# Two-layer hybrid encoder trunk on one Trainium2 core: residual quarters loaded one a unit from GpSimd's queue, every second early gate/up weight through other buffers, the second meta substitution placed later

## The chip, the cores and the metric

The kernel runs on one core of a Trainium2 chip. The metric is the device time of one execution in microseconds (us). Engines are named as in the profile: PE is TensorE (matmul; PEld its weight loads), DVE is VectorE, ACT is ScalarE, POOL is GpSimd, SP is SyncE, which here only issues DMAs. DMAs are issued from three queues: SP's (nearly all), ACT's, and POOL's. [...]

## The reference, cut to what matters

Sixteen learned meta tokens are put ahead of 1024 tokens, so that the sequence has L = 1040 columns; the model width is 1024. Two layers follow:

```python
for l in range(DEPTH):
    h = h + hybrid_mixer(rmsnorm(h, norm1_w[l]), w_in[l], conv_qkv_w[l], ...)
    h = h + swiglu(rmsnorm(h, norm2_w[l]), w_gate_up[l], w_down[l])
h = rmsnorm(h, final_norm_w)
return h[:, N_META:]
```

The mixer has a bidirectional gated-delta-rule part (4 heads of 128, worked in chunks, which needs the inverse of a triangular matrix for each chunk, head and direction) and a gated short convolution. SwiGLU is `(silu(h @ gate) * (h @ up)) @ w_down` with an inner width of 2816 = 22 tiles of 128. All inputs are float32.

## The kernel before, in words

**Precision and layout.** Activations lie transposed, channels on the 128 partitions and tokens along the free axis. Each float32 operand of a large product is split into a high part (a rounded copy made by ACT) and a low part (the difference, made by DVE or POOL), and three matmuls are added up: high x high, high x low, low x high. Such a triple stands at L157 to L159 (`dense`), L1021 to L1023 (`prod`, for gate/up) and L1441 to L1443 (down projection).

**The planner.** The kernel is written in a framework that allots buffers, sets semaphores and plans the order of each engine's list: it goes through a simulated timeline with modelled durations and picks by priority among what is ready. Priorities follow the order of the program except where the kernel sets them itself. Tiles with a tag share a fixed number of buffers: `raw` has 2 (weights just loaded), `whi` and `wlo` 3 each (split weights), `ck2` has 5 (tiles of 2 KB a partition for many uses). A tile waits until one of its buffers has been released. `after(ins, prev)` adds a dependency by hand.

**Mixer.** While the query projections run, `chunk_p` (L442) computes for each of nine chunks c the decayed k-k products of both directions d, and `k_out` (L418) transposes k for the chunk on PE (L424), copies it into a `ck2` tile `kt` on ACT (L426) and stores it (L427). One `k_out` and one `chunk_p` are worked after each third of a projection. For chunk 0, the 16 meta tokens, the triangular system is solved by `meta()` (L464): a store to DRAM and two loads on SP (L468 to L470), 30 small operations on POOL (L474 and L475), and a store and a load on SP (L476 and L477). It holds two `ck2` tiles. Layer 0 has one for each direction, both at chunk 0; layer 1 needs only d = 0. `query_lengths` (L608) sends sums through DRAM into the `ck2` tile `rows` with POOL DMAs (L617, L618), and PE transposes it.

**Output projection and early gate/up.** The output projection goes over 8 row tiles in two halves of the columns (`out_part`, L947), its weights loaded through `raw`. The gate/up product is a Strassen-like scheme with seven products for four blocks. Two of the products of the first four of 22 tiles f are worked early, during and after the output projection: `early_part(f, q)` (L1047) loads a weight of 256 KB into a `raw` tile (L1050), splits it (L1003 on ACT, L1004 on DVE) and multiplies. Besides these, DVE then forms sums of the normalised activations (L983) and their low parts (L971).

**Gate/up.** For each f four weights are loaded, two into `raw` and two into `ck2` (L1288 to L1291), and combined on DVE (L1296 to L1301).

**Down projection.** Also with seven products (P5, P3, P2, P1, P6, P7, P4), worked in 84 units (p, b, m): for each product, three blocks b of three inner tiles, and four row tiles m. A unit has 9 triples' worth of matmuls: 18 matmuls of 260 columns in layer 0, 9 of 512 in layer 1. Weights are prepared five units ahead (`LEAD`, L1202, L1203, with sums at L1160 and L1199), activations are loaded back from DRAM (L1222) into a ring of seven parts and split (L1250, L1251; a difference at L1253). Many DVE operations are tied behind the addition of two units earlier (`behind`). After the last block a product is added to the residual `hr` (L1447), which must have been loaded by then: the quarter (a row tile's half of the columns, 256 or 260 KB) is loaded from `hd` at L1421, in the units with b = 1 of the products P5, P3, P2 and P7: 16 loads a layer, which have no dependency but the room and go out on SP as soon as the planner finds a place.

Of the kernel before, what the change touches and what calls it, by code (L numbers as in the profile page):

```python
# [17 lines left out]
L = 1040  # L18
# [24 lines left out]
def trunk(ctx: ExitStack, tc: tile.TileContext, xT, w_in, w_ba, w_out, w_gu, w_dn,  # L43
          par_d, alog_d, dtb_d, cst_d, eye_d, out):
    nc = tc.nc
# [16 lines left out]
    def t2k(tag):  # L62
        return sb.tile([128, 4, 128], F32, tag="ck2", bufs=5, name=nm(tag))
# [25 lines left out]
    def after(ins, prev):  # L89

        if prev is not None:
            tc.add_manual_dep(ins.ins, prev.ins.name, dep, reason="order")
        return ins
# [4 lines left out]
    mm = nc.tensor.matmul  # L98
# [5 lines left out]
    dma = nc.sync.dma_start  # L104
    adma = nc.scalar.dma_start
    qdma = nc.gpsimd.dma_start
# [125 lines left out]
    for m in range(KT):  # L232
        cs = FULL if m == 0 else [(0, L)]
# [46 lines left out]
    for l in range(DEPTH):  # L280
# [6 lines left out]
        o0 = 16 if last else 0  # L287
# [32 lines left out]
        hd = dram.tile([KT, 128, L], F32, name=nm("hd"))  # L320
# [117 lines left out]
            return (16, 0) if c == 0 else (128, 16 + 128 * (c - 1))  # L438

        ptm = []  # L440

        def chunk_p(c):  # L442

            if not Pd:
                Pd.extend(sb.tile([128, 4 * L], F32, tag=f"P{d}", name=nm("P")) for d in range(2))
                Pv.extend(p[:, 0:4096].rearrange("p (q i) -> p q i", i=128) for p in Pd)
                p_ = sb.tile([128, 4 * L], F32, tag=Y[0][2], name=nm("ptm"))
                ptm.extend(p_[:, 512 * i:512 * i + 512].rearrange("p (h i) -> p h i", h=4) for i in range(8))
            n, s0 = span(c)
            kk = bank("b").rearrange("p (h i) -> p h i", h=4)  # L450
            for h in range(H):
                mm(kk[0:n, h, 0:n], KTt[:, h, s0:s0 + n], KTt[:, h, s0:s0 + n], start=True, stop=True)
            for d in (dirs0 if c == 0 else (0, 1)):
                gr = ptm[(2 * c + d) % 8]
                adma(gr[0:n, :, 0:n], gd[36 * d + 4 * c:36 * d + 4 * c + 4, 0:n].partition_broadcast(n))
                for h in range(H):
                    stt(out=gr[0:n, h, 0:n], in0=gr[0:n, h, 0:n], scalar=nGb[0:n, d, c, h:h + 1], in1=off[0:n, d, 0:n], op0=ALU.subtract, op1=ALU.add)
                act(out=gr[0:n, :, 0:n], in_=gr[0:n, :, 0:n], func=AF.Exp, scale=-1.0)
                adma(dtd[c, d].rearrange("p (h i) -> p h i", h=4)[0:n, :, 0:n], gr[0:n, :, 0:n])
                dst = P0[d] if c == 0 else Pv[d][:, 4 * c - 4:4 * c, :]  # L460
                tt(out=dst, in0=kk[0:n, :, 0:n], in1=gr[0:n, :, 0:n], op=ALU.mult)
                if c == 0:

                    def meta():  # L464
                        mt = t2k("mt").rearrange("p a b -> p (a b)")[0:4].rearrange("p (w a b) -> p w a b", w=2, a=16)
                        Wm, Zm = mt[:, 0], mt[:, 1]
                        Tm = t2k("mt").rearrange("p a b -> p (a b)")[0:4, 0:256].rearrange("p (a b) -> p a b", a=16)
                        dma(m0d[d, 0].rearrange("h j i -> j h i"), P0[d])  # L468
                        dma(Wm, m0d[d, 0])
                        dma(Zm, eye_d[0:4, :, :][:, 0:16, 0:16])  # L470
                        for s in (range(15, 0, -1) if d == 0 else range(0, 15)):
                            r0, r1, a0, a1 = (0, s, s, 16) if d == 0 else (s + 1, 16, 0, s + 1)
                            sh = [4, r1 - r0, a1 - a0]
                            ptt(out=Tm[:, r0:r1, a0:a1], in0=Wm[:, r0:r1, s:s + 1].to_broadcast(sh), in1=Zm[:, s:s + 1, a0:a1].to_broadcast(sh), op=ALU.mult)  # L474
                            ptt(out=Zm[:, r0:r1, a0:a1], in0=Zm[:, r0:r1, a0:a1], in1=Tm[:, r0:r1, a0:a1], op=ALU.subtract)  # L475
                        dma(m0d[d, 1], Zm)  # L476
                        dma(P0[d], m0d[d, 1].rearrange("h j i -> j h i"))  # L477

                    meta()

        def chunk_a(c):

# [125 lines left out]
        def query_lengths(l2):  # L608


            r4 = t2k("r4").rearrange("p a b -> p (a b)")[:, 0:260]
            nc.vector.tensor_copy(r4, l2[:, 0:260])
            for h in range(H):
                qdma(rnd[h].rearrange("(a c) -> a c", a=4), r4.rearrange("(a b) c -> a b c", b=32)[:, h, :])
            rows = t2k("rows").rearrange("p a b -> p (a b)")[0:36, 0:128]
            for h in range(H):
                qdma(rows[9 * h:9 * h + 1, 0:16], rnd[h:h + 1, 0:16])  # L617
                qdma(rows[9 * h + 1:9 * h + 9, :], rnd[h, 16:L].rearrange("(c p) -> c p", p=128))  # L618

            def turn():  # L620
                ps = pa()
                low(lambda: nc.tensor.transpose(ps[:, 0:36], rows, ident[0:36, 0:36]))
                ts(out=g[:, 0].rearrange("p c h -> p h c"), in0=ps[:, 0:36].rearrange("p (h c) -> p h c", h=4), scalar1=HD * EPS, scalar2=HD * EPS * EPS, op0=ALU.mult, op1=ALU.add)

            jobs.append(turn)
# [258 lines left out]
        for i, (d, s) in enumerate(order):  # L884
            at_prio(base - 17000 + 4000 * (1 - d) + 400 * s)
            c = s if d == 0 else 8 - s
# [7 lines left out]
        hr = [hb[m // 4][:, m % 4, :] for m in range(KT)]  # L894
# [43 lines left out]
        def half(ap, z):  # L938

            v = ap.rearrange("p (g e) -> p g e", g=4) if len(ap.shape) == 2 else ap.rearrange("p k (g e) -> p k g e", g=4)  # L940
            s = slice(1, 3) if z == 0 else slice(0, 4, 3)
            return v[:, s, :] if len(ap.shape) == 2 else v[:, :, s, :]
# [70 lines left out]
        CW = E if E * 4 > 1024 else NB  # L1013
# [11 lines left out]
        def raw4(tag):  # L1025
            if tag == "raw":
                return wp.tile([128, WK, 128], F32, tag="raw", bufs=2, name=nm("raw"))
            return t2k("rw")
# [17 lines left out]

        def early_part(f, q):  # L1047

            A = raw4("raw")
            dma(A, w_gu[l, f, 0, :, 4 * q:4 * q + 4, :])  # L1050
            w = w_op(A, True)
            if q == 0:
                early[f] = (row(Y[1], F32, 3), row(X[1], F32, 3)) if f < 3 else (row(Y[1] + "f"), c4k())
                bks0[f] = [pbank() for j in range(NJ)]
            for j in range(NJ):
                prod(bks0[f][j], w, T[("B11", "B21")[q]], j, q == 0)
                act(out=part(early[f][1 - q], 0, j), in_=pin(bks0[f][j]), func=AF.Copy)  # L1057
# [12 lines left out]
        for m in range(KT + 2):  # L1070
# [7 lines left out]
            k = m - 2  # L1078
# [9 lines left out]
            else:  # L1088
                c = pcol(P_N2 + k)
# [171 lines left out]
        for t in range(4, NP * 7):  # L1261
            u = max(0, 4 * (t // 3 - 1) - 1 + t % 3)
# [23 lines left out]
        for f in range(FT):  # L1286
# [21 lines left out]
            g, u = early[f] if f < NE else (row((X[1], Y[1])[f % 2] + "f"), row(X[1], F32, 3))  # L1308
            ps = {}
# [99 lines left out]
              "P6": (0, 1, ALU.add), "P7": (1, 1, ALU.add), "P4": (1, 0, ALU.add)}  # L1409

        FIRST = {"P2": (0, 0), "P5": (1, 1), "P3": (0, 1), "P7": (1, 0)}
        bks = {}
        for i in range(NF):
            u = (42, 44, 46, 70)[i]
            under[u - 3].append(lambda i=i: plain_load(i))
            under[u].append(lambda i=i: plain_row(i))
        for u, (p, b, m) in enumerate(UNITS):
            if b == 1 and p in FIRST:
                dh, z = FIRST[p]
                q = 4 * dh + m  # L1420
                dma(half(hr[q][:, o0:L], z), half(hd[q][:, o0:L], z))  # L1421
            at[0] = u
            for fn in under[u]:
                fn()
            if last and u == 77:
                for q in range(KT):
                    last_weights(q)
            if not last and u >= len(UNITS) - 2:
                pre["dn", u - len(UNITS) + 2] = wload(w_dn[l, u - len(UNITS) + 2, :, 0:NF, :], NF)
            if p in ("P5", "P2", "P1") and b == 0:  # L1430
                for j in range(NJ):
                    bks[m, j] = pbank()
            wh, wl = dw.pop(("w", u))
            for j in range(NJ):
                ps = bks[m, j]
                cs = slice(CW * j, CW * j + CW)
                for k in range(3):
                    th, tl = t_slot(3 * (u // 4) + k)
                    st = p in ("P2", "P5", "P1") and b == 0 and k == 0
                    en = b == NBK - 1 and k == 2  # L1440
                    mm(ps[:, :CW], wh[:, k, :], th[:, cs], start=st, stop=False, skip_group_check=True)  # L1441
                    mm(ps[:, :CW], wh[:, k, :], tl[:, cs], start=False, stop=False, skip_group_check=True)  # L1442
                    mm(ps[:, :CW], wl[:, k, :], th[:, cs], start=False, stop=en, skip_group_check=True)  # L1443
                if b == NBK - 1:
                    dh, z, op = TO[p]
                    h = part(hr[4 * dh + m], z, j)
                    read_out[u] = tt(out=h, in0=pin(ps), in1=h, op=op)  # L1447
# [136 lines left out]
```

## Time and profile before

| | |
|---|---|
| median of 3 runs | 2505.1 us (2501.76 to 2505.31) |
| the profiled execution | 2502.22 us |
| its span, first to last instruction | 2500.1 us |
| granted TensorE clock, mean | 0.997 |
| DMA over the span | 335.26 MB, mean 134 GB/s |

A profile shows one execution. "Busy" is the time in which an engine worked on an instruction; the waits list gives for each group of instructions who released it, the total in us, how often, and the longest. In a list of DMAs the time to landing goes from issue to the last byte. The table of windows gives the busy us of each engine in a stretch of time, with the number of instructions in brackets, then the granted clock of PE (1 is full), the busy share of the 16 DMA engines, and GB/s.

### The profile page before, as it was taken

The numbers are of one execution on the slowest core, as the hardware profiler recorded it, in microseconds if no ns is written. First come the engines' busy times: TensorE is split into PE (matmuls) and PEld (weight loads), VectorE is DVE, ScalarE is ACT, GpSimd is POOL, SyncE is SP. The second block draws the span as 40 slices with busy tenths as digits, with TensorE's granted clock in tenths as the row PEclk, the third lists the DMA queues.
The fourth block names the chain that finished last, engine by engine and source line by source line (L and its number), as shares of the span: only waits on it lengthen the run. The fifth ranks groups of instructions, "written<-read, shape, count | busy, mean of one in ns | idle before, by whom it ended". The sixth has DMA issues, their size and how long they took to land. (4 is left out here: it accounts for less than half of the span.)

```text
span 2500.1 us, 44874 instructions
## 1 busy us (share of the span) xinstructions
PE 2461.5 (98%) x17508; PEld 2257.4 (90%) x17508; DVE 1693.0 (68%) x3073; ACT 1045.0 (42%) x1944; POOL 339.3 (14%) x359
## 2 busy tenths in 40 slices
PE   8999999999999999999999999999999999999998
PEld 6989999999999999999999888998978888887887
DVE  4788333659877777877656893336698777678765
ACT  5554333535333333344444543335453333234444
POOL 2031212431000000000120212132400000000012
PEclk9999999999999999999999999999999999999999
DMA  3444353523323332764224443445342233238531
GB/s 130 134 166 152 119 163 135 201 85 130 117 102 103 109 102 82 253 200 138 84 86 139 160 145 127 151 134 206 118 133 97 89 115 116 92 114 272 178 119 68
DMA packets 199529, 335.26 MB, mean 134 GB/s; under 512 B 23404, under 2 KB 85668, under 8 KB 199316
## 3 DMA queue, kind: packets, MB, share of 16 engines
q1 hardware_dynamic: 171204, 293.84, 35.3%
q10 hardware_dynamic: 25936, 34.19, 4.2%
q0 software_dynamic: 2176, 4.36, 0.5%
q8 instruction: 137, 2.24, 0.4%
q14 instruction: 76, 0.62, 0.1%
HBM read 250.31 MB, written 81.99 MB: 133 GB/s over the span
## 5 line engine op out<-in xcount | busy, mean ns | idle before, releaser
L131 POOL TENSOR_TENSOR wlo<-raw,whi 128x512 fp32r<-128x512 f32 x132 | 176.5, 1339 | 1267.8 <-ACT whi L130 1125.9
L157 PE MATMUL pacc<-a,whi 128*128 128x346 f32 (+1 forms) x808 | 264.5, 330 | 8.3 <-ACT whi L130 7.4
L159 PE MATMUL pacc<-a,wlo 128*128 128x346 f32 (+1 forms) x808 | 263.5, 327 | 1.1 <-POOL wlo L131 0.6
L157 PE MATMUL pacc<-b,whi 128*128 128x346 f32 (+2 forms) x672 | 234.5, 349 | 0.7 <-ACT whi L130 0.7
L159 PE MATMUL pacc<-b,wlo 128*128 128x346 f32 (+2 forms) x672 | 232.4, 347 | 0.9 <-DVE wlo L131 0.8
L158 PE MATMUL pacc<-a,whi 128*128 128x346 f32 (+1 forms) x688 | 225.8, 328 | 0.0
L158 PE MATMUL pacc<-b,whi 128*128 128x346 f32 (+2 forms) x580 | 200.7, 346 | 0.4 <-DVE b L907 0.3
L130 ACT ACTIVATE whi<-raw 128x512 fp32r<-128x512 f32 x168 | 105.8, 630 | 221.6 <-PE pacc L158 105.5
L157 PEld LDWEIGHTS pacc<-a,whi 128*128 128x128 f32 x808 | 152.8, 190 | 13.6 <-ACT whi L130 7.9
L159 PEld LDWEIGHTS pacc<-a,wlo 128*128 128x128 f32 x808 | 153.3, 190 | 2.6 <-POOL wlo L131 1.1
L157 PEld LDWEIGHTS pacc<-b,whi 128*128 128x128 f32 x672 | 126.4, 188 | 12.4 <-issue 3.1
L159 PEld LDWEIGHTS pacc<-b,wlo 128*128 128x128 f32 x672 | 126.3, 188 | 10.6 <-DVE wlo L131 1.0
L158 PEld LDWEIGHTS pacc<-a,whi 128*128 128x128 f32 x688 | 130.6, 190 | 2.9 <-issue 2.6
L158 PEld LDWEIGHTS pacc<-b,whi 128*128 128x128 f32 x580 | 109.2, 188 | 8.0 <-issue 0.9
L1003 ACT ACTIVATE whi<-rw 128x512 fp32r<-128x512 f32 x92 | 57.6, 631 | 137.7 <-PE pf L1022 36.4
L1003 ACT ACTIVATE b<-rw 128x512 fp32r<-128x512 f32 x64 | 39.9, 631 | 135.2 <-PE pacc L1022 37.7
L296 DVE TENSOR_TENSOR a<-pacc,rstd 128x346 f32<-128x346 f32 (+2 forms) x59 | 32.7, 555 | 85.4 <-PE pacc L159 85.4
L131 POOL TENSOR_TENSOR a<-raw,a 128x512 fp32r<-128x512 f32 x3 | 3.9, 1287 | 595.0 <-ACT a L130 595.0
L1003 ACT ACTIVATE a<-rw 128x512 fp32r<-128x512 f32 x64 | 40.0, 629 | 101.8 <-PE pacc L1022 62.3
L296 DVE TENSOR_TENSOR b<-pacc,rstd 128x346 f32<-128x346 f32 (+1 forms) x63 | 32.5, 515 | 72.5 <-PE pacc L159 72.5
L1004 DVE TENSOR_TENSOR wlo<-rw,whi 128x512 fp32r<-128x512 f32 x92 | 62.8, 685 | 2.9 <-ACT whi L1003 2.1
L1021 PE MATMUL pacc<-b,whi 128*128 128x260 f32 (+1 forms) x172 | 52.7, 306 | 0.7 <-ACT b L1057 0.7
(966 smaller groups left out, 8010.7 us busy)
## 6 DMA issues: line engine op xcount, KB each, us to landing
raw<-in_w_in SPq DMA_DIRECT2D x112, 256.0 KB, 2.9
raw<-in_w_gu SPq DMA_DIRECT2D x104, 256.0 KB, 3.0
rw<-in_w_gu SPq DMA_DIRECT2D x88, 256.0 KB, 3.1
rw<-in_w_dn SPq DMA_DIRECT2D x94, 192.0 KB, 2.7
rec<-vkd SPq DMA_DIRECT2D x61, 256.0 KB, 2.8
raw<-in_w_out SPq DMA_DIRECT2D x48, 256.0 KB, 2.7
b<-ad SPq DMA_DIRECT2D x45, 260.0 KB, 3.4
a<-ad SPq DMA_DIRECT2D x45, 256.0 KB, 5.2
```

Of the source, the lines that this page charges most:

```text
L130: whi_done[0] = act(out=hi, in_=raw[:, 0:kk, :], func=AF.Copy)
L131: (tt if lov[0] else ptt)(out=lo, in0=raw[:, 0:kk, :], in1=hi.bitcast(F32), op=ALU.subtract)
L157: mm(ps[:, :n], wh, xh[:, n0:n1], start=(k == 0), stop=False)
L158: mm(ps[:, :n], wh, xl[:, n0:n1], start=False, stop=False)
L159: mm(ps[:, :n], wl, xh[:, n0:n1], start=False, stop=(k == K - 1))
L296: tt(out=t[:, n0:n1], in0=ps, in1=rstd[:, n0:n1], op=ALU.mult)
L1003: act(out=hi, in_=src, func=AF.Copy)
L1004: tt(out=lo, in0=src, in1=hi.bitcast(F32), op=ALU.subtract)
L1021: mm(ps[:, :CW], w[0][:, k, :], th[:, cs], start=first and k == 0, stop=False, skip_group_check=True)
```

## The change

1. The residual quarters are issued from POOL's queue instead of SP's, and the one of unit u waits (by a dependency added by hand) for the first matmul of unit u - 2.
2. `early_part` loads the weights with q = 1 into a `ck2` tile instead of a `raw` tile: four of eight in each layer.
3. In layer 0 `meta()` for d = 1 is worked after chunk 5 instead of at chunk 0; that for d = 0 comes after both directions of chunk 0. In layer 1 the one that there is stays at chunk 0.
4. The tile `rows` is set to zero by POOL before it is filled.

```diff
         ptm = []
+        metas = []
...
-                    def meta():
+                    def meta(d=d):
...
-                    meta()
+                    metas.append(meta)
+            if c in (0, 5) and metas:
+                metas.pop(0)()
...
             rows = t2k("rows").rearrange("p a b -> p (a b)")[0:36, 0:128]
+            nc.gpsimd.memset(rows, 0.0)
...
         def early_part(f, q):
-            A = raw4("raw")
+            A = raw4(("raw", "ck2")[q])
...
-        bks = {}
+        bks, begun = {}, {}
...
-                dma(half(hr[q][:, o0:L], z), half(hd[q][:, o0:L], z))
+                after(qdma(half(hr[q][:, o0:L], z), half(hd[q][:, o0:L], z)), begun[u - 2])
...
-                    mm(ps[:, :CW], wh[:, k, :], th[:, cs], start=st, stop=False, skip_group_check=True)
+                    one = mm(ps[:, :CW], wh[:, k, :], th[:, cs], start=st, stop=False, skip_group_check=True)
+                    begun.setdefault(u, one)
```

`qdma` is the DMA start of POOL, `dma` that of SP.

## The prediction

> **What bounds the kernel now.** I read the page first, then the waits of PE, the chain of waits near the longest of them, and the busy time of each engine there.
>
> ```profile
> span 2500.1 us, 44874 instructions
> ...
> PE 2461.5 (98%) x17508; PEld 2257.4 (90%) x17508; DVE 1693.0 (68%) x3073; ACT 1045.0 (42%) x1944; POOL 339.3 (14%) x359
> ```
>
> PE works 2461.5 of 2500.1 us, so all its idle time is 38.6 us. The change takes no matmul away; it can only shorten waits, and what it may win stands in the waits of PE (total, times, longest, in us):
>
> ```profile
> PE pacc L157 <- ACT whi L130: 9.6, 5, 5.8
> PE pf L1441 <- ACT a L1202: 3.8, 1, 3.8
> PE pf L1021 <- ACT whi L1003: 1.7, 1, 1.7
> ...
> PE pa L1443 <- DVE b L1203: 1.4, 1, 1.4
> ...
> PE pa L424 <- ACT kt L426: 1.2, 2, 1.0
> ```
>
> The 5.8 us is the start of the kernel and stays. The second row lies in the down projection of layer 1, just after the residual quarters are loaded; the fourth in that of layer 0; the third to the early gate/up weights of layer 0; L424 to the transposes of k beside the meta substitution. All four places are touched. The longest wait seen closely, in PE's timeline (start, duration) and in the busy time by window (length, PE, PEld, DVE, ACT, POOL, granted clock, DMA share, GB/s):
>
> ```profile
> 2291.05 0.39 PE L1441 MATMUL pacc<-P,a 128*128 128x512 f32 x1
> 2291.28 0.40 PE L1442 MATMUL pacc<-P,a 128*128 128x512 f32 x1
> 2295.49 0.50 PE L1441 MATMUL pf<-P,a 128*128 128x512 f32 x1 [3.81 <-ACT a L1202]
> ...
> 2296.32 0.63 PE L1441 MATMUL pacc<-P,a 128*128 128x512 f32 x1
> ...
> 2299.70 0.39 PE L1441 MATMUL pacc<-P,a 128*128 128x512 f32 x1
> ```
>
> ```profile
> 2260.00:2288.00 28.00, 28.00 (x122) 22.55 (x121) 23.45 (x42) 9.98 (x17) 0.00 (x0) 1.00 1.03 352
> ...
> 2296.00:2300.00 4.00, 4.00 (x12) 3.15 (x12) 4.00 (x10) 1.75 (x4) 0.00 (x0) 0.57 0.59 167
> 2300.00:2400.00 100.00, 100.00 (x431) 80.50 (x430) 74.75 (x130) 48.61 (x90) 0.00 (x0) 1.00 0.54 169
> ```
>
> Normal matmuls start 0.23 us apart. After the 3.81 us wait the granted clock falls to 0.57 and the eight matmuls from 2296.32 to 2299.70 take 3.38 us instead of 8 x 0.23 = 1.86: 1.5 us more, in which PE counts as busy. The wait really costs 3.8 + 1.5 = **5.3 us**.
>
> Its cause: the DMA engines are full (share 1.03, 352 GB/s) from 2260 to 2288. The chain of waits and DVE's timeline name what suffered, SP's timeline what stood ahead of it:
>
> ```profile
> 2275.75 5.64 DMA a<-ad
> ```
>
> ```profile
> 2281.41 0.69 DVE L1253 TENSOR_TENSOR a<-a,a 128x512 f32<-128x512 f32 x1 [4.52 <-DMA a<-ad]
> ```
>
> ```profile
> 2270.58 4.70 SPq L1421 DMA_DIRECT2D b<-hd  x8
> ```
>
> ```profile
> L1421 SPq DMA_DIRECT2D a<-hd x16: 319/359/715, 1040.7 to 1052.4; - x16
> L1421 SPq DMA_DIRECT2D b<-hd x16: 319/346/655, 2263.6 to 2276.4; - x16
> ```
>
> ```profile
> b<-hd SPq DMA_DIRECT2D x16, 256.0 KB, 5.3
> ```
>
> All 16 residual quarters go out in 13 us: 16 x 256 KB = 4.2 MB, or 11.9 of the 28 full us at 352 GB/s. The activation load a<-ad stands behind the last eight in SP's queue and then lands in 5.64 us. DVE idles 4.52 us for it, then works without a pause until PE has starved.
>
> **The change part by part.**
>
> *Residual quarters, layer 1.* They become POOL DMAs, one a unit, each behind the first matmul of two units earlier. Only units 4 to 7 lie in the full stretch; the other 12 (3.1 MB, 8.9 us at that rate) go to units 16 to 19, 28 to 31 and 64 to 67, where the share is 0.54. SP loses the 4.70 us ahead of a<-ad, and a less crowded load lands sooner:
>
> ```profile
> DMA to landing us min/median/max: 3.0/3.5/5.6
> ```
>
> This is L1222's row, all 90 activation loads. At 3.5 instead of 5.64 us and only 2.4 us earlier the 4.52 us would be covered, and I expect more than that. Gain 5.3 (bounds 0, if buffers and not the queue held the load, and 5.3).
>
> What is late next? The quarters themselves, perhaps. POOL's loads in this trace, with their landing times, and the first matmul of the down projections:
>
> ```profile
> L415 POOL DMA_DIRECT2D bc<-rnd x8: 527/536/568, 95.9 to 1357.7; - x8
> ...
> DMA to landing us min/median/max: 4.0/6.3/7.9
> ```
>
> ```profile
> L1441 PE MATMUL pf<-P,whi x123: 278/284/396, 1037.5 to 2430.2; 128*128 128x260 f32 x93, 128*128 128x512 f32 x30
> ...
> L1441 PE MATMUL pa<-P,whi x54: 392/394/399, 2254.5 to 2434.3; 128*128 128x512 f32 x54
> ```
>
> A unit of layer 1 is nine matmuls, 2.1 us. Unit 4's quarter is free to go when unit 2 begins, at 2254.5 + 4.2 = 2258.7, and is first added after unit 8, at 2254.5 + 9 x 2.1 = 2273.4: 14.7 us for a load that took at most 7.9 at twice the size. POOL has no work here (0.00 in the windows), so 0.54 us of issue each costs nothing, and behind the waiting DMA stands only the next quarter.
>
> *Residual quarters, layer 0.* The same burst lies ahead of the 1.4 us wait of L1443 (PE resumes at 1071.9), but in the twelve us before it DVE waits for nothing and is simply late:
>
> ```profile
> 1060.00:1072.00 12.00, 10.58 (x89) 10.37 (x87) 12.00 (x26) 3.68 (x7) 0.00 (x0) 1.00 0.64 208
> ```
>
> Bounds 0 and 1.4; I take 0.4, nearer to nothing, because no DMA row stands before it.
>
> *Early weights.* 16 loads (8 a layer) share two raw buffers, each waiting for the one two before. Half now use ck2, which has five and is free after the scan. ACT waits for such a load, and PE for ACT:
>
> ```profile
> 599.22 0.63 ACT L1003 ACTIVATE whi<-raw 128x512 fp32r<-128x512 f32 x1 [2.17 <-DMA raw<-in_w_gu]
> ```
>
> ```profile
> 599.90 0.39 PE L1021 MATMUL pf<-b,whi 128*128 128x260 f32 x1 [1.74 <-ACT whi L1003]
> ```
>
> ```profile
> 590.00:623.00 33.00, 30.25 (x247) 28.97 (x246) 31.04 (x44) 19.53 (x37) 1.43 (x1) 1.00 0.32 109
> 1816.00:1856.00 40.00, 36.56 (x191) 28.86 (x190) 39.66 (x57) 23.67 (x37) 3.56 (x2) 1.00 0.36 121
> ```
>
> PE idles 2.75 us in the first stretch and 3.44 in the second. But DVE has only 1.96 and 0.34 us to spare, and the second stretch ends in a wait for it:
>
> ```profile
> 1855.89 0.50 PE L1023 MATMUL pa<-P,b 128*128 128x512 f32 x1 [0.51 <-DVE b L1004]
> ```
>
> So most of a removed wait comes back as a wait for DVE. I take 1.2 us in layer 0 (bounds 0 and 2.75) and 0.3 in layer 1 (0 and 3.44). The first gate/up tiles find their ck2 buffers taken by early weights, but these have been split before they are needed; costed at nothing, and at most one landing of 3.5 us if that is wrong.
>
> *Second meta substitution, layer 0.* Each holds two of the five ck2 buffers, both together four, so the transposed k go through one:
>
> ```profile
> ACT kt L426 <- DMA vkd<-kt: 3.3, 3, 2.0
> ```
>
> ```profile
> 143.31 0.66 PE L424 MATMUL pa<-ident,b 128*128 128x128 f32 x4 [0.98 <-ACT kt L426]
> ...
> 161.54 0.43 PE L157 MATMUL pacc<-a,whi 128*128 128x348 f32 x1 [1.04 <-ACT whi L130]
> ```
>
> With the second one five chunks later three buffers serve k in between. ACT's 3.3 us go, PE's 1.2 at L424 with them, and ACT reaches the weight of 161.54 earlier. Its POOL work and its four transfers on SP move too:
>
> ```profile
> 126.59 0.21 POOL L474 TENSOR_TENSOR mt<-mt 4x15 f32<-4x15 f32 x1 [18.35 <-DMA mt<-m0d]
> ...
> 143.91 1.31 POOL L475 TENSOR_TENSOR mt<-mt,mt 4x15 f32<-4x15 f32 x1
> ```
>
> ```profile
> 142.32 3.20 SPq L476 DMA_DIRECT2D m0d<-mt  x2
> ...
> 163.67 7.81 SPq L129 DMA_DIRECT2D raw<-in_w_in  x4
> ```
>
> Two took 18.6 us, one takes 9.3. If it begins near 143 its last store holds SP until about 156; the next weight goes out at 163.67, so 7 us of cover remain. Its result is read only at the end of the backward scan. Gain 1.1 (bounds 2.3 and, if SP still stood there at 163.67, minus 2). In layer 1 there is one substitution, and its place is the same.
>
> *The memset of rows* runs on POOL while it waits for the lengths to land (up to 1.5 us):
>
> ```profile
> L617 POOLq EVENT_SEMAPHORE  x5: 17/17/1506, 166.9 to 1419.4; - x5
> ```
>
> No row shows it; between nothing and one POOL wait of 1.5 us. I take 0.
>
> *What the planner does with it.* The order on every engine is planned from modelled times, and taking 32 DMAs out of SP's list moves others. No trace shows the new order: between -3 and +5 us, about two or three waits like those above. I charge 0.7, the size of one.
>
> **Sum:** 5.3 + 0.4 + 1.2 + 0.3 + 1.1 - 0.7 = 7.6 us off. The profiled execution took 2502.2 us (span 2500.1), 2.9 below the median 2505.1; the four times known average 2503.6. The change acts on any of them: 2494.6 from the profiled one, **2496.0** from the average, which I take.
>
> [...]
>
> **Rivals.**
>
> *The wait stays in part.* The full stretch goes on to 2288, twelve us after the last quarter, and DVE has a backlog of its own: buffers freed by DVE may have held a<-ad, not SP. Against it: the chain leads through that one landing. Half the cure with the small terms gives about 2 + 1.5 - 0.7: 2500 to 2503, no measurable change.
>
> *The quarters come late from POOL* (slower). The place is the first addition after unit 8. If a quarter takes over 14.7 us, DVE, which works strictly in order, stands before it, the weights of the units after it are not split, and with a lead of five units (10.5 us) PE stops. For it: the DMA engines are full just there, and the loads now share them with SP's. Each us beyond 14.7 is a us of DVE, and DVE's 4.52 us cost PE 3.8 and the slow clock 1.5, so a quarter 5 to 6 us late in both layers costs 2 x (5 to 6) + 2 x 1.5 = 13 to 15 us against the 7.6 of the sum: 2509 to 2511. It decides from a landing of some 18 us, where the loss equals the gain. Against it: 7.9 us was the most that any POOL load took. [...]
>
> *The new order costs more than it saves.* The planner's list for SP or DVE puts an activation load or a split later, at the same down projection or at the scan; three or four waits of 1 to 4 us, one with the slow clock: 2503 to 2511.
>
> **How the numbers follow.** Forecast 0.56 (2490 to 2500); wait stays in part 0.18; late quarters 0.08; new order 0.18, a third of it within 0.2%. 0.2% is 5 us, about what a measurement of this kernel can tell from no change. Faster: 0.56 + 0.01 = 0.57. Same: 0.17 + 0.06 = 0.23. Slower: 0.08 + 0.12 = 0.20. The forecast's own range reaches down to 2490 if the early weights give all 6.2 us. The 8-in-10 range takes in the partial cure and most of the new order: 2489 to 2508.
>
> **What would show it.** In the new profile: no block of hd loads near 2263 and 1040, but single ones on POOL; L1253 no longer waiting 4.5 us for a<-ad; no PE wait at L1441 over 1 us and no window at clock 0.57 near 2296; L1003 waits of PE under 1 us but a longer one for DVE before 625 and 1856; no ACT wait of kt for vkd. I am wrong if L1447 waits for a<-hd or b<-hd, if L1441 still waits some 3 us, or if new waits stand outside these places.

## The result and the profile after

The changed kernel takes 2498.3 us, median of 14 runs (2497.08 to 2502.03). The kernel before took 2504.31 us on the same chip (14 runs, 2496.85 to 2509.04); the ratio is 0.9982, 95% interval 0.9975 to 0.9989 (the two medians alone give 0.9976). A second series gave 0.9987 (0.9978 to 0.9996). So by the ratios the change is faster by 0.13 to 0.18%: the sign was right and the time lies in the forecast's own range, 2490 to 2500, but the gain is smaller than the 0.2% that the prediction set as its bound for no change, and the forecast of 2496.0 was 2.3 us too low.

The page of the changed kernel:

```profile
span 2495.8 us, 44963 instructions
...
PE 2459.7 (99%) x17508; PEld 2258.6 (90%) x17508; DVE 1689.5 (68%) x3073; ACT 1043.2 (42%) x1944; POOL 359.5 (14%) x393
```

PE's idle time is 36.1 us, 2.5 less than before. PE's busy time fell too, by 1.8 us with the same 17508 matmuls: part of the gain may be slow clock that went (the window 2296 to 2300 below). The waits of PE:

```profile
PE pacc L157 <- ACT whi L130: 8.9, 5, 5.8
...
PE pacc L1025 <- ACT b L1061: 1.2, 1, 1.2
PE pa L1025 <- ACT b L1007: 1.2, 1, 1.2
PE pa L708 <- DVE vm L701: 1.1, 1, 1.1
PE pf L588 <- ACT a L592: 1.1, 1, 1.1
PE pb L1025 <- ACT a L1007: 1.1, 1, 1.1
PE pb L1027 <- DVE a L1008: 1.1, 1, 1.1
```

(Line numbers are up to 5 higher than before: L1025 to L1027 is the gate/up triple, L1445, L1447 and L1448 the triple of the down projection, L1452 the addition to the residual, L1007 and L1008 the split.) The 3.8 us of the down projection, the 1.4 us of that in layer 0 and the 1.7 us of the early weights are gone from the list, and of the 1.2 us of the transposed k 0.2 are left. In their place stand waits of about 1.1 us, in the early gate/up work (L1025, L1027) and in the mixer of layer 1 (L708, L588). The busy time in the same windows as before:

```profile
1060.00:1072.00 12.00, 12.00 (x103) 12.00 (x102) 12.00 (x27) 5.73 (x12) 2.17 (x3) 1.00 0.60 190
2260.00:2288.00 28.00, 28.00 (x122) 22.56 (x121) 25.39 (x45) 10.51 (x20) 3.36 (x5) 1.00 0.71 220
2296.00:2300.00 4.00, 4.00 (x19) 3.20 (x18) 4.00 (x8) 1.06 (x3) 0.00 (x0) 1.00 1.05 353
2300.00:2400.00 100.00, 100.00 (x431) 80.53 (x430) 75.09 (x131) 48.07 (x89) 4.33 (x8) 1.00 0.61 192
```

In the 28 us after 2260 the DMA share fell from 1.03 to 0.71, and in the next 100 it rose from 0.54 to 0.61: the quarters have been spread. The window 2296 to 2300 has 19 matmuls at clock 1.00, where it had 12 at 0.57; its DMA share is 1.05, so a full stretch of that length did not hold PE up here. The DMA list and POOL's timeline show the quarters in their new place:

```profile
a<-hd POOLq DMA_DIRECT2D x16, 260.0 KB, 4.6
b<-hd POOLq DMA_DIRECT2D x16, 256.0 KB, 4.7
```

```profile
2262.49 0.84 POOL L1425 DMA_DIRECT2D b<-hd  x1 [436.49 <-DMA a<-ad]
2264.59 0.74 POOL L1425 DMA_DIRECT2D b<-hd  x1 [1.26 <-PE pacc L1445]
```

They go out 2.1 us apart, one a unit, and land in 4.6 and 4.7 us (medians), far from the 14.7 that were to spare. L1452, which adds the quarters, waits for none of them. The difference that waited 4.52 us before (L1253, now L1257) starts without a wait; from 2254 to 2300 DVE waits for one activation load only, 1.3 us for an early one, at 2255.74:

```profile
2274.34 0.70 DVE L1257 TENSOR_TENSOR a<-a,a 128x512 f32<-128x512 f32 x1
```

```profile
DVE a L1257 <- DMA a<-ad: 1.3, 1, 1.3
```

One line was not expected. It is a drain among POOL's last instructions, at the end of the program (the columns are minimum, median and longest of its drains in ns). Before, and after:

```profile
L1579 POOLq DRAIN  x3: 40/102/4799, 2494.3 to 2499.9; - x3
```

```profile
L1584 POOLq DRAIN  x3: 40/98/7418, 2487.6 to 2495.5; - x3
```

The longest drain grew by 2.62 us, and the program ends behind it: from PE's last matmul to the end of the span the time is 2.6 us longer than before.

### The profile page after: what moved, and what is told of

Read it like the earlier page. It is cut to its first block, busy times and chain, and to the rows that moved or that the text cites. A ratio compares the mean times of both kernels' runs of the same rounds, so it can differ in the third digit from the quotient of the medians.

```text
span 2495.8 us, 44963 instructions
## 1 busy us (share of the span) xinstructions
PE 2459.7 (99%) x17508; PEld 2258.6 (90%) x17508; DVE 1689.5 (68%) x3073; ACT 1043.2 (42%) x1944; POOL 359.5 (14%) x393
## 5 line engine op out<-in xcount | busy, mean ns | idle before, releaser
L1007 ACT ACTIVATE whi<-rw 128x512 fp32r<-128x512 f32 x100 | 62.6, 629 | 141.6 <-PE pf L1026 36.8
L1007 ACT ACTIVATE b<-rw 128x512 fp32r<-128x512 f32 x64 | 40.0, 631 | 133.7 <-PE pacc L1026 39.4
L1425 POOL DMA_DIRECT2D a<-hd x16 | 10.2, 640 | 576.3 <-DMA rw<-in_w_dn 450.8
L1425 POOL DMA_DIRECT2D b<-hd x16 | 10.2, 641 | 558.2 <-DMA a<-ad 436.5
L1007 ACT ACTIVATE a<-rw 128x512 fp32r<-128x512 f32 x64 | 40.0, 629 | 97.8 <-PE pacc L1026 64.1
L1008 DVE TENSOR_TENSOR wlo<-rw,whi 128x512 fp32r<-128x512 f32 x100 | 68.3, 685 | 2.5 <-ACT whi L1007 2.1
```

The lines of the kernel that those rows point to most:

```text
L1007: act(out=hi, in_=src, func=AF.Copy)
L1008: tt(out=lo, in0=src, in1=hi.bitcast(F32), op=ALU.subtract)
```

## The experiments

All ratios are to the kernel before on the same chip, with 5 to 12 runs of each. The rows were taken on three chips (the first four on one; both SP rows without early weights, the unspaced one and the last on another; the other two on a third), so small differences between ratios of different chips say little.

| kernel | median us | ratio, 95% interval |
|---|---|---|
| residual part alone (POOL, spaced) | 2497.8 | 0.9984 (0.9976 to 0.9993) |
| early weights alone | 2499.92 | 0.9996 (0.9987 to 1.0005) |
| meta part and memset alone | 2499.59 | 0.9994 (0.9985 to 1.0002) |
| residual and meta, without early weights | 2493.46 | 0.9970 (0.9958 to 0.9982) |
| residual spaced, on SP's queue | 2496.93 | 0.9971 (0.9959 to 0.9982) |
| residual on POOL's queue, not spaced | 2505.71 | 1.0011 (1.0002 to 1.0020) |
| residual spaced, POOL in layer 1, SP in layer 0 | 2495.44 | 0.9972 (0.9961 to 0.9984) |
| residual spaced on SP, and meta | 2492.69 | **0.9955 (0.9941 to 0.9968)** |
| whole change, quarters on SP | 2495.87 | 0.9972 (0.9962 to 0.9983) |
| whole change, early low parts on POOL | 2506.17 | 1.0013 (1.0004 to 1.0021) |

To see where each gained, I read from PE's timelines when the same matmuls start and end, and took for each stage its length less that of the first profile of the kernel before (us; each stage counts from its own start; the first 106 us, which moved by -1.3 to +1.2, and the 137 us between the two layers, which moved by 0.1, are left out; "end" runs from the last matmul of the down projection to the end of the span).

| kernel | mixer 0 | output to gate/up 0 | down 0 | mixer 1 | output to gate/up 1 | down 1 | end | span |
|---|---|---|---|---|---|---|---|---|
| before, second profile | -1.5 | +1.7 | 0.0 | -1.3 | +0.9 | +0.9 | +0.1 | 2501.1 |
| residual alone | +0.2 | +1.5 | -1.7 | +0.1 | 0.0 | -5.6 | +2.4 | 2498.0 |
| early alone | -2.3 | -0.1 | +1.9 | -2.0 | +0.1 | -0.2 | +0.3 | 2497.5 |
| meta alone | -2.8 | +1.3 | +1.2 | -0.3 | -0.7 | 0.0 | +0.1 | 2497.6 |
| residual and meta | -2.7 | 0.0 | -1.7 | -3.1 | -1.6 | -5.6 | +3.2 | 2488.9 |
| spaced on SP | +0.8 | -0.1 | -1.8 | -1.0 | +1.6 | -5.6 | 0.0 | 2494.6 |
| POOL, not spaced | -0.1 | +1.5 | +3.3 | -2.2 | -1.5 | +0.3 | +2.4 | 2504.6 |
| POOL in layer 1 only | +0.1 | +0.9 | -1.7 | -0.6 | -0.9 | -5.6 | +1.9 | 2494.2 |
| spaced on SP, and meta | -3.6 | +1.2 | -1.7 | -2.7 | -0.5 | -5.6 | 0.0 | 2487.5 |
| whole change, SP | -2.5 | +1.3 | -1.7 | +2.5 | -0.2 | -5.6 | 0.0 | 2495.1 |
| **whole change** | -2.5 | +0.7 | -1.7 | +2.0 | -0.7 | -5.6 | +3.3 | 2495.8 |
| whole change, second profile | -3.4 | +1.4 | -1.8 | +2.3 | -0.1 | -5.6 | +2.3 | 2495.3 |
| whole change, low parts on POOL | -3.2 | +3.3 | +1.2 | -0.8 | +4.5 | -5.6 | +3.1 | 2503.3 |

**How far one program moves.** The kernels before and after were profiled a second time, unchanged.

> The kernel before, unchanged, profiled a second time, to see how far the stages of one program move from one execution to the next. Theory A (the differences of 1 to 3 us between kernels in the mixers and around the norm's statistics come from the planned order, which is fixed for each kernel): every stage of the second profile within 0.5 us of the first. Rival B (they are the variation of executions, whose times spread over 8 us): single stages that no edit touches move by 1 to 3 us between the two profiles of the same kernel, the mixer of layer 1 and the stretch before the norm's statistics among them.

> The whole change, unchanged, a second time. Theory A (planned order): the mixer of layer 1 is again 2.5 us longer than in the first profile of the kernel before, the down projections again 5.6 and 1.7 us shorter. Rival B (variation): the down projections keep their gain, but the mixer of layer 1 is off by 1 us or more from the first profile of the change. Either way the drain of POOL is 7.42 us and the ratio 0.998.

The second profile of the kernel before took 2502.89 us. Its stages differ by up to 1.7 us from the first, without any edit: rival B holds for differences of that size, and single ones under 2 us in the table say nothing. Its large wait was there again, now 4.11 us instead of 3.81:

```profile
2295.74 0.80 PE L1441 MATMUL pf<-P,a 128*128 128x512 f32 x1 [4.11 <-ACT a L1202]
```

The second profile of the change repeats both down projections (-1.8, -5.6), the drain (7.42 us) and the longer mixer of layer 1 (+2.3): those come from the program, as theory A has it. (Its single other stages differ by up to 1.0 us from the first profile of the change.)

**The parts one by one.**

```diff
-                dma(half(hr[q][:, o0:L], z), half(hd[q][:, o0:L], z))
+                after(qdma(half(hr[q][:, o0:L], z), half(hd[q][:, o0:L], z)), begun[u - 2])
```

> Only the residual quarters are changed (POOL's queue, one a unit); early weights and meta substitution as before. Theory A (the spread loads are the whole of the gain that counts): the 3.8 us wait of PE in the down projection of layer 1 and the 1.4 us one in layer 0 are gone, no stretch at clock 0.57 there; from the first matmul of the down projection to the last one, layer 1 is 5.6 us shorter than before (175.7 to about 170.1) and layer 0 1.7 us shorter; all other stages within 1 us; time 5 to 8 us under the kernel before. Rival B (the parts share the gain, and the early weights carry some of it): 2 to 4 us under.

```diff
-            A = raw4("raw")
+            A = raw4(("raw", "ck2")[q])
```

> Only every second early gate/up weight goes through the other buffers. Theory A (VectorE is full there, so a removed wait comes back as a wait for VectorE): PE's waits for the early weights (2.75 us in layer 0, about 2.9 in layer 1) shrink, but new waits for DVE or for weights behind DVE of the same size stand at the first gate/up tiles; time within 2 us of the kernel before. Rival B: the stage is 2 to 5 us shorter in the two layers together, and the time 2 to 5 us under.

```diff
-                    meta()
+                    metas.append(meta)
+            if c in (0, 5) and metas:
+                metas.pop(0)()
...
+            nc.gpsimd.memset(rows, 0.0)
```

> Only the second meta substitution is placed later (with the memset of rows that goes with it). Theory A: the waits for the transposed k near 143 us (0.98 and 0.25) are gone, the mixer of layer 0 is 1 to 2.6 us shorter, and layer 1's mixer is as long as before, because nothing of it is changed there; time 1 to 3 us under. Rival C (this part moves layer 1's mixer too, through the memset or the buffers that it shifts): layer 1's mixer is 1.5 to 3 us longer, with new PE waits of about 1.1 us near the transposes of v and the inversion, and the time is as before.

The next one has the first and the third edit without the second.

> The change without the early weights. Theory A: as fast as the whole change or up to 2 us faster, since the early part cost layer 0 0.8 us and gave layer 1 little: 5 to 8 us under the kernel before. Rival B: 2 to 4 us slower than the whole change.

The residual part alone gives the whole gain of the change, 0.9984: -1.7 and -5.6 us in the down projections, and 2.4 us lost again at the end. Theory A had 5 to 8 us there; with the loss at the end, which it did not have, it is 4. The other two alone can't be told from no change, though the meta part shortens the mixer of layer 0 in every kernel that has it: by 2.5 to 3.6 us in seven profiles, mean 3.0, against -2.3 to +0.8 in the six profiles without it (mean -0.5). Residual and meta together, 0.9970, are at least as fast as all three; the intervals overlap, so that alone does not yet settle that the early weights cost something.

**Queue or spacing?** The quarters stay on SP's queue, but spaced; or go to POOL's, but unspaced.

```diff
-                dma(half(hr[q][:, o0:L], z), half(hd[q][:, o0:L], z))
+                after(dma(half(hr[q][:, o0:L], z), half(hd[q][:, o0:L], z)), begun[u - 2])
```

> Only the residual part of the change, and of that only the spacing: each quarter waits for the first matmul of two units earlier, but it stays on SP's queue. Theory A (the burst fills the DMA engines and stands ahead of the activation load; spacing alone cures it): DVE's wait for a<-ad at the difference stays under 1 us, PE's waits of 3.8 and 1.4 us go, down projection of layer 1 is 5.6 us shorter and that of layer 0 1.7 us; and since no quarter is issued by POOL, POOL's last drain is 4.8 us as before, not the 7.42 us of the three kernels with POOL quarters, so span about 2492.8, ratio 0.996 to 0.998. Rival B (SP's in-order queue was the trouble, and a quarter that waits there for a matmul holds up the activation loads behind it): new waits of DVE for a<-ad of over 1 us, down projection no shorter than before, ratio 0.999 or more.

```diff
-                dma(half(hr[q][:, o0:L], z), half(hd[q][:, o0:L], z))
+                qdma(half(hr[q][:, o0:L], z), half(hd[q][:, o0:L], z))
```

> Only the residual part, and of that only the queue: the quarters go out from POOL, with no dependency, so in bursts of 16 as before. Theory A (spacing is what cures): the DMA engines are again full for over 20 us near the start of the down projection of layer 1, the activation load lands in over 4.5 us, a PE wait of 1 us or more stays there; POOL's last drain is 7.42 us, the tail 2.5 us longer; 2502 to 2506, ratio 1.000 to 1.002. Rival B (the relief of SP's queue is what cures): no PE wait over 0.5 us there, down projection of layer 1 shorter by 5 us, ratio as that of the spaced POOL quarters, 0.998.

Spacing is what cures. Spaced on SP: the same -1.8 and -5.6 us, DMA share 0.75, no loss at the end.

```profile
2260.00:2288.00 28.00, 28.00 (x122) 22.57 (x121) 25.58 (x45) 10.60 (x19) 0.00 (x0) 1.00 0.75 239
```

In bursts from POOL the down projections are no better than before (+3.3 and +0.3). Its window, DVE's waits in that stretch and PE's timeline:

```profile
2260.00:2288.00 28.00, 27.54 (x119) 21.91 (x118) 21.21 (x37) 9.58 (x17) 10.20 (x16) 1.00 0.98 341
```

```profile
DVE a L1253 <- DMA a<-ad: 7.0, 2, 5.9
```

```profile
2297.98 0.65 PE L1444 MATMUL pacc<-P,a 128*128 128x512 f32 x1 [2.88 <-DVE a L1203]
```

Nothing of the quarters stands in SP's list any more, and yet DVE waits 5.9 us for one a<-ad. The load that is waited for can be followed, first with bursts from POOL, then spaced on SP:

```profile
2274.20 0.38 SPq L1222 DMA_DIRECT2D a<-ad  x1
2283.18 0.69 DVE L1253 TENSOR_TENSOR a<-a,a 128x512 f32<-128x512 f32 x1 [5.85 <-DMA a<-ad]
```

```profile
2272.48 0.36 SPq L1222 DMA_DIRECT2D a<-ad  x1
2275.53 0.68 DVE L1253 TENSOR_TENSOR a<-a,a 128x512 f32<-128x512 f32 x1
```

Counted from the projection's first activation load, SP issued it 22.4 us later in the kernel before, and 19.7 to 20.0 us later in both of these and in the whole change. So the burst in SP's list did cost it some 2.5 us. But with that list clear and the DMA engines as full as before (0.98), DVE had it only 9.0 us after its issue, against 5.64 us to landing before; with spaced quarters it was used 3.0 to 3.1 us after its issue, without a wait. The crowd on the DMA engines is enough for the wait, and the order in SP's queue was not needed for it. The quarters themselves land in 6.8 to 7.6 us here (medians of the two layers) instead of 4.6.

**The end.** The quarters of layer 1 from POOL, those of layer 0 from SP, all spaced:

```diff
-                dma(half(hr[q][:, o0:L], z), half(hd[q][:, o0:L], z))
+                after((qdma if l else dma)(half(hr[q][:, o0:L], z), half(hd[q][:, o0:L], z)), begun[u - 2])
```

> Only the residual part, spaced in both layers, from POOL in layer 1 and from SP in layer 0: POOL issues 16 quarters instead of 32 or none. Theory A (the last drain grows with the number of POOL's transfers: 4.80 us with none of the quarters, 7.42 with 32, 0.082 us each): 6.11 us, and the ratio between those of spaced SP and spaced POOL quarters, 0.997 to 0.998. Rival B (the drain has two values, with and without late POOL transfers): 7.42 or 4.80 us.

```profile
L1580 POOLq DRAIN  x3: 40/93/6116, 2487.3 to 2494.0; - x3
```

4.80 us without quarters, 6.12 with 16, 7.42 with 32: 0.082 us for each transfer, as theory A said. Why it grows is not shown. The value is the same to 0.01 us in all seven profiles without and all six with 32 of them, however late or early these were. From PE's last matmul to the end it is 1.3 us more here, 2.4 to 2.6 with 32.

**The best combination, and the early weights in company.** Spaced on SP, with the meta part; and the same with the early weights, which is the whole change but for the queue.

> Spaced quarters on SP's queue, the second meta substitution after chunk 5, and the memset; the early weights as before. By the sum of stages measured one by one: -5.6 and -1.7 (down projections), -2.8 (mixer of layer 0), tail 0: span near 2490, ratio 0.995 to 0.997, which would be faster than the whole change. Rival (the queue or the planner's order eats it): ratio 0.998 or more, with new PE waits in the mixer of layer 1 or in a down projection.

> The whole change, but the spaced quarters stay on SP's queue: against the spaced quarters with the meta part alone (ratio 0.9955) it differs by the early weights only, and against the whole change by the queue only. Theory A (the early weights through other buffers neither gain nor cost, since DVE works without a pause there; the tail of 2.6 us is POOL's drain): 2.6 us under the whole change, drain 4.80 us, ratio 0.9955 to 0.997. Rival B (the early part costs some 3 us in company with the others): ratio 0.997 to 0.998, and PE waits of over 1 us for ACT and DVE near 616 and 1834 us.

Without the early weights the ratio is 0.9955, the fastest of all: 0.45% of 2502.7 or some 11 us, where the change took off 3 to 4.5. Of PE's waits of before, those of the early weights remain (the first 1.7 us again), and none in either down projection:

```profile
PE pf L1025 <- ACT whi L1007: 1.7, 1, 1.7
```

With the early weights it is 0.9972, as rival B has it (the two intervals overlap, the two spans are 7.6 us apart); against the second series of the whole change, on the same chip, it is 3.6 us faster by the medians, with the drain back at 4.80 us. The PE waits of 1.1 and 1.2 us that rival B named are there. But the early stage itself is as long in both (+1.2 and +1.3). What differs is the mixer of layer 1, +2.5 instead of -2.7, where nothing was edited. There PE stands before a transpose, in the whole change with SP and in the second profile of the whole change:

```profile
PE pa L708 <- DVE vm L701: 3.1, 1, 3.1
```

```profile
1476.44 0.66 PE L708 MATMUL pa<-ident,a3f 128*128 128x128 f32 x4 [3.19 <-DVE vm L701]
```

and then the clock falls:

```profile
1476.00:1480.00 4.00, 3.56 (x17) 3.57 (x18) 3.61 (x9) 2.62 (x4) 1.13 (x1) 0.70 0.43 127
```

The wait is a matter of the planned order. On PE this transpose comes after 11881 matmuls in the kernel before, after 11872 without the early weights, and after 11861 with them and the rest; DVE's copy `vm`, which it waits for, has moved the other way, two steps of the triangular solve later. The stage's length follows this place: the seven profiles with 11881 lie between -1.3 and +0.1, the two with 11872 at -3.1 and -2.7, the three with 11861 at +2.0 to +2.5. The early weights alone (11876, -2.0) do not lengthen it. (With bursts from POOL the list differs more, 11565, and the stage stands at -2.2.) In the kernel with spaced SP and meta the same wait is 0.3 us. In the first profile of the change it was 1.1 us, with two other waits of 1.1 and 0.7 us beside it.

**Is the early stage bound by DVE?** The whole change, with DVE relieved of the low parts of the early weights.

```diff
-            tt(out=lo, in0=src, in1=hi.bitcast(F32), op=ALU.subtract)
+            (ptt if early else tt)(out=lo, in0=src, in1=hi.bitcast(F32), op=ALU.subtract)
```

> The whole change, with the low parts of the early gate/up weights (16 a kernel) made by POOL (1.34 us each in this trace's rows) instead of DVE (0.69 us). Theory A (the early stage is bound by DVE, which is why the early weights through other buffers gained nothing there): the PE waits near 616 and 618 us (1.1 us each, behind DVE's weight sums) go, the stretch from the norm's statistics to the down projection of layer 0 is at least 1.5 us shorter, ratio 0.996 to 0.998. Rival B (the bound is elsewhere, or POOL's slower operation is now what PE waits for): waits of the same size or PE waits for POOL's wlo, ratio 0.998 to 1.000.

It is slower than before, 1.0013: +3.3 us in layer 0 and +4.5 in layer 1. (The +1.2 of its down projection in layer 0 belongs to this loss: PE has no wait there, but the last gate/up matmuls, up to 1041.8 us, lie behind the first of the down projection, at 1038.5.) DVE was not relieved. Its timeline and POOL's:

```profile
595.67 1.82 POOL L1008 TENSOR_TENSOR wlo<-rw,whi 128x512 fp32r<-128x512 f32 x1 [3.86 <-ACT whi L1007]
596.26 1.79 DVE L178 SCALAR_TENSOR_TENSOR b<-a,par,b 128x520 fp32r<-128x520 f32 x1
597.45 1.75 POOL L1008 TENSOR_TENSOR wlo<-raw,whi 128x512 fp32r<-128x512 f32 x1
...
598.31 1.42 DVE L1300 TENSOR_TENSOR rw<-rw,rw 128x512 f32<-128x512 f32 x1
```

In the changed kernel the same two DVE operations took 0.75 and 0.68 us:

```profile
595.68 0.75 DVE L178 SCALAR_TENSOR_TENSOR b<-a,par,b 128x520 fp32r<-128x520 f32 x1
...
600.72 0.68 DVE L1300 TENSOR_TENSOR rw<-rw,rw 128x512 f32<-128x512 f32 x1
```

So beside a POOL operation of 1.8 us, meant to save DVE 0.69, the DVE operation took 1.04 and 0.74 us longer; each of the two ends some 0.5 us after POOL's. Why they took longer is not shown. The stretch of 40 us, in the changed kernel and in this one:

```profile
585.00:625.00 40.00, 36.86 (x299) 35.18 (x298) 39.22 (x59) 24.20 (x45) 2.15 (x1) 1.00 0.35 111
```

```profile
585.00:625.00 40.00, 33.20 (x252) 31.18 (x251) 38.44 (x46) 22.17 (x42) 14.30 (x8) 0.96 0.26 82
```

DVE did 46 operations in its 38.4 busy us instead of 59 in 39.2, and PE worked 3.7 us less. Neither theory forecast that; the experiment did not relieve DVE but slowed it. Read that way it bears theory A out in part: DVE still has hardly a pause (1.6 us of 40), and what it is late with, PE lacks. A relieved DVE was not tried.

## Why the prediction was right or wrong, point by point

- **Residual quarters, layer 1:** 5.3 us forecast, 5.6 measured, in all profiles with spaced quarters. The mechanism was half right. The full DMA engines held the activation load, as the prediction said (9.0 us from issue to use at a share of 0.98, 3.0 to 3.1 with spaced quarters); the quarters ahead of it in SP's list, which it named beside them, delayed the load by some 2.5 us, near the 2.4 of the prediction, but did not decide (spaced on SP cures as well, POOL in bursts does not). The landing of 3.5 us that the prediction set against 5.64 is not that of "all 90 activation loads": the trace holds the landing of seven of them, three in layer 1 (5.6, 5.2 and 3.2 us). The 3.0 us from issue to use in the changed kernel bear the value out all the same.
- **Residual quarters, layer 0:** 0.4 forecast, 1.7 measured. The term was mis-sized, and its upper bound of 1.4 with it. The twelve us that the prediction read showed DVE without a pause; the pause was just ahead of them. In the five us before, DVE was busy for 3.20 of 5.00 us in the kernel before and 4.72 after, with the DMA share at 1.06 and 0.82 (first row before, second after):

```profile
1055.00:1060.00 5.00, 5.00 (x44) 5.00 (x43) 3.20 (x7) 0.95 (x2) 0.00 (x0) 1.00 1.06 387
```

```profile
1055.00:1060.00 5.00, 5.00 (x44) 5.00 (x44) 4.72 (x11) 0.53 (x1) 0.00 (x0) 1.00 0.82 267
```

  What ended these pauses before were matmuls of PE (0.4 to 0.65 us each, at the additions), not a load, so the way from the burst to the pause isn't shown. That spacing cures it is: PE's wait there was 1.4 to 3.2 us in the five profiles with unspaced quarters, and none is left in the nine with spaced ones.

- **Early weights:** 1.5 us forecast, nothing measured in their own stage, as far as its scatter of up to 1.7 us lets one say (alone they took 0.04% off, interval -0.13 to +0.05%). The step that failed is "so most of a removed wait comes back as a wait for DVE": all of it came back. The stretch of 40 us before the change:

```profile
585.00:625.00 40.00, 37.04 (x303) 35.64 (x302) 38.04 (x56) 24.53 (x46) 2.13 (x1) 1.00 0.33 111
```

  PE's idle time there was 2.96 us, and 3.14 after (its row stands above); DVE's busy time rose from 38.04 to 39.22. PE waits 1.1 us for ACT's split and 1.1 for DVE's, and ACT waits for DVE's weight sums instead of the load:

```profile
ACT a L1007 <- DVE rw L1301: 1.5, 1, 1.5
```

- **Second meta substitution:** 1.1 forecast (bounds 2.3 and -2). ACT's wait for the store of the transposed k is gone in all seven profiles that have the meta part. Mixer 0 is 2.5 us shorter by the means of the table. That is more than the wait; the rest isn't settled. The granted clock from 219 to 223 us, in the same mixer, was 0.50 and 0.65 in the two profiles of the kernel before and 1.00 with the early weights alone, so part of the differences there is clock and not order. It was 1.00 in only one of the seven profiles with the meta part (0.59 to 0.69 in the others), so this clock isn't what sets them apart.
- **The planner's order:** 0.7 forecast, as a guess; 2.0 to 2.5 us in the mixer of layer 1 (about 5 against the best kernel). This was the third rival's mechanism, an untouched stage whose order turned worse, though its place (DVE's copy `vm` behind the solve) was not the one named. New waits outside the places that were named are also one of the prediction's own signs of being wrong, and this one came true.
- **The end:** nothing forecast, 2.6 us measured. The prediction costed POOL's queue by its issues and landings alone; the drain behind the last instruction was in the profile of before (4.80 us) and was not read.
- **Memset:** nothing forecast and nothing seen; it was not run alone.
- **The rivals:** quarters from POOL did not come late: 4.6 us against 14.7. Their issues, with DVE busy beside them, took 0.65 us (median, in ns below), 0.84 at most:

```profile
L1425 POOL DMA_DIRECT2D a<-hd x16: 537/646/834, 1040.8 to 1176.0; - x16
L1425 POOL DMA_DIRECT2D b<-hd x16: 537/644/839, 2262.5 to 2393.9; - x16
```

  No wait stayed in part with spaced quarters. With bursts from POOL 2.88 us were left and the slow clock with them (0.57 over four us), so no run shows the half of the cure that the first rival counted with. That DVE works in order, as the second rival has it, is seen at one place of the kernel before: DVE stood 2.44 us for a copy (L697, at 227.24 us), and a subtraction whose inputs it had itself finished at 224.80 (L525) came only behind it, at 227.45.

Added up by the table, the measured terms are -5.6, -1.7, 0, -2.5, +2.3 (mixer 1) and +2.6 (end): -4.9 us, where the two profiles of the change give -4.3 and -4.8, and the forecast had -7.6. The sign came out right because the one large term was right; half of what was won, 9.8 us, was given back by two terms, of which one had not been read and one was a guess. That the forecast came so near is luck in part: the terms for the quarters and the meta substitution were too small by 3.0 us together, and those for the early weights, the order and the end too favourable by 5.7.

## What to carry to other kernels

When a wait falls on a load, look at the DMA share before looking at the queue: here spacing 16 transfers by 2 us cured it from either queue, and moving them without spacing made it no better. Each small gain in such a tuned kernel must be read on an engine that has time to spare; where DVE was busy for 38 of 40 us, a removed ACT wait showed no gain. And before a queue is used for more transfers, read what the program's last instructions wait for, since it can be added to every run, as the 2.5 us were here.

## What was not expected of the hardware

- POOL's last drain took 4.80 us without the quarters, 6.12 with 16 and 7.42 with 32 transfers issued by POOL, though the last of them had landed some 90 us earlier (the last issue stands at 2393.9 us). Whether it counts transfers or their packets isn't told apart: all quarters are of nearly the same size.
- Two DVE operations with two inputs, each beside a POOL operation that also has two, took 0.74 and 1.04 us longer than in the changed kernel.
- The clock fell after shorter waits than the 3.81 us of the prediction. After the 3.19 us in the mixer of layer 1 it was 0.70 over four us; after the 2.88 us in the kernel with bursts from POOL it was 0.57:

```profile
2298.00:2302.00 4.00, 4.00 (x11) 3.13 (x12) 4.00 (x9) 1.11 (x3) 0.00 (x0) 0.57 0.75 236
```

  After the 1.4 us wait in the down projection of layer 0 it stayed at 1.00. Nor does the length of the wait alone decide: in the mixer of layer 0 the clock was 0.50 from 219 to 223 us in the kernel before, behind a wait of 1.55 us amid 32x32 matmuls, 1.00 in the same place with the early weights alone, and 1.00 over the four us behind the wait of 1.74 us in the early gate/up work of the same kernel (599.90 to 603.90 us).
